# RWKV-7 stage of a two-layer trunk: sample states in four transfers each way, systems loaded one item earlier, a third raw weight buffer, and another order within a step

## The chip, the cores and the metric

The kernel runs on one core of a Trainium2 chip. The metric is the device time of one execution in microseconds (us); the smaller the better. Times of several runs are given by their median. A core has TensorE (PE in the profile; its weight loads are PEld), VectorE (DVE), ScalarE (ACT), GpSimd (POOL) and SyncE (SP). In this kernel SP does nothing but issue DMAs, one after the other in the order of its queue, and an entry whose data or buffer isn't ready holds up all that stand behind it.

## The reference

One inference step of a two-layer trunk, for a prompt of 1024 tokens with 16 learned ones ahead of it, and for 8 samples of 8 tokens each that continue from stored states. Each layer is x = x + mixer(rmsnorm(x)). Layer 0 is a gated DeltaNet. Layer 1, in which the change lies, is RWKV-7 time mixing, 16 heads of 64:

```
xs = xn + (xprev - xn) * mu                      # six mixes of a token with the one before
r, k, v, z = xs[:4] @ w_rkvz
w = -softplus(-(w0 + tanh(xs[4] @ w1) @ w2)) - 0.5 ;  a = sigmoid(a0 + (xs[5] @ a1) @ a2)
kk = l2norm(k * k_k) ;  k = k * (1 + (a - 1) * k_a) ;  decay = exp(-exp(w)) ;  b = kk * a
for each token t, each head:                     # state S is [value, key]
    S = S * decay_t + (S @ -kk_t) b_t^T + v_t k_t^T
    y_t = S @ r_t
y = groupnorm(y) * lnx_w + lnx_b + sum(r * k * r_k) * v
out = (y * silu(z)) @ w_o
```

The final states are outputs too: one for the prompt (p_rwkv) and one for each sample (s_rwkv, 8 samples x 16 heads x 64 x 64 numbers).

## The kernel before

The tokens of both inputs stand in 1104 columns, cut into three segments of 384, 384 and 336; the 64 sample tokens are the first chunk of segment 0. Float32 matmuls are split: a value x becomes a high part (a cast on ACT, "whi" or "yh", line 86) and a low part (a subtraction on POOL, "wlo" or "yl", line 90), and three matmuls take the place of one.

The last stage of the program, `wave`, runs the recurrence of layer 1 with its output projection. It starts at about 1857 us and goes on to the end. Its unit is an item: n = 8s + p, segment s and pair of heads p, 24 in all, each with 6 chunks of 64 tokens. A loop over steps tau starts a new item every second step; an item is active for six steps, so three items are worked on at a time. A step does, for the chunks of the active items: the part that depends on the old state (`step_solve`, which ends with X on DVE, line 1497, and its copy on ACT, line 1499), the solve by the chunk's precomputed triangular system (`step_inner`, matmuls rX and rS from X and rTT), then `step_old`, `step_state` (new state, output y) and the statistics of y. Between them `fill` puts matmuls that don't depend on the recurrence: the gate projection z (zz, layer 1's w_z) at first, then the output projection (zo and do, with w_o) of finished segments.

Each item is prepared by `rwkv_front`, ahead of its steps: input loads (tau = 2n-5), decays (2n-4), a third part in which r*k*r_k is split (2n-3), and six "parts" with scores, keys, values and the bonus term (2n-2 and 2n-1). The item's systems come from memory into rTT, 128 x 384 numbers, by one DMA (line 1360), which is issued with the values part at tau = 2n-1, into one of three buffers, n mod 3; the item's first use of it is at tau = 2n.

The eight items of segment 0 hold the samples as their first chunk. `rwkv_sample_read` loads the pair's 8 x 2 states (sn, eight DMAs of 64 x 2 x 64, line 1608), transposes them on PE (dsn), copies them to Sb on ACT, multiplies them with the chunk's vectors (drsr) and copies the transposed product on DVE (xss, line 1631), which X needs. `rwkv_sample_write` masks the chunk's vectors (ue, line 1638), multiplies (drsw, line 1643), adds that to Sb and scales it on DVE (lines 1645 and 1646), transposes back (dsbT), copies (ssn, ACT) and stores with eight DMAs (line 1656). The PSUM tiles of dsn, drsr, drsw and dsbT share one pool of two buffers ("d"); the second drsr group is in one of its own and the first shares the tile of the first product.

Weights of the gate and output projections come through `stream`: 72 chunks of up to 512 x 128, loaded five ahead into two raw buffers (wraw, line 204), split into whi and wlo three ahead.

`rwkv_finish` normalises y (the four and two ACT operations at line 62 of "y"), transposes it (fyT), adds the bonus and multiplies by the gate (k and lz on DVE, lines 1587 and 1588) and splits the result (yh, yl) for the projection, in pieces that `wave` calls at tau-6, tau-7 and tau-8.

On PE and ACT the instructions stand in the order in which the code is written (`manual_schedule`). On DVE, POOL and SP a planner sets the order from the dependences and its own estimates.

Of the kernel before, what the change touches and what calls it, by code (L numbers as in the profile page):

```python
# [35 lines left out]
class Builder:  # L36
# [8 lines left out]
    def t(self, pool, shape, tag, bufs=1, dt=F32):  # L45
        self.uid += 1
        return pool.tile(shape, dt, name=f"{tag}_{self.uid}", tag=tag, bufs=bufs)
# [144 lines left out]
    def open_weights(self, ctx):  # L192
        self.wp = ctx.enter_context(self.tc.tile_pool(name="weights", bufs=1))

    def load_w(self, src, kt=8, into=None, later=False):

        nc = self.nc
        n = src.shape[1]
        v = src.rearrange("(k p) m -> p k m", p=128)
        his, los = [], []  # L200
        for h in range(0, kt, 4):
            w = self.t(self.wp, [128, 4, 128], "wraw", 2)
            m = min(4, kt - h)
            nc.sync.dma_start(w[:, 0:m, 0:n], v[:, h:h + m, :])
            if later:
                return w, m, n
            if into:
                hi, lo = into[0][h // 4], into[1][h // 4]
            else:
                hi = self.t(self.wp, [128, 4, 128], "whi", 3, F32R)  # L210
                lo = self.t(self.wp, [128, 4, 128], "wlo", 3, F32R)
            self.split(w[:, 0:m, 0:n], hi[:, 0:m, 0:n], lo[:, 0:m, 0:n], eng_lo="dve" if into else "pool")
            his.append(hi)
            los.append(lo)
        return his, los

    def stream(self, srcs):

        raw, w = [], []
        for n in range(len(srcs)):  # L220
            while len(raw) < min(n + 5, len(srcs)):
                q = len(raw)
                if q > 1 and len(w) < q - 1:
                    x, m, c = raw[len(w)]
                    hi, lo = (self.t(self.wp, [128, 4, 128], a, 3, F32R) for a in ("whi", "wlo"))
                    self.split(x[:, 0:m, 0:c], hi[:, 0:m, 0:c], lo[:, 0:m, 0:c])
                    w.append((hi, lo))
                raw.append(self.load_w(srcs[q], srcs[q].shape[0] // 128, later=True))
            while len(w) < min(n + 3, len(srcs)):
                x, m, c = raw[len(w)]  # L230
                hi, lo = (self.t(self.wp, [128, 4, 128], a, 3, F32R) for a in ("whi", "wlo"))
                self.split(x[:, 0:m, 0:c], hi[:, 0:m, 0:c], lo[:, 0:m, 0:c])
                w.append((hi, lo))
            yield w[n]
# [1114 lines left out]
    def rwkv_front(self, p, s):  # L1349

        nc, t, ap, fp, col = self.nc, self.t, self.ap, self.fp, self.pcol
        P = Ctx()
# [3 lines left out]

        P.TT = self.TTz[P.n % len(self.TTz)]

        def system():
            nc.sync.dma_start(P.TT.rearrange("p c k -> p (c k)"), self.ttd[(P.n + 1) // 5][:, 384 * (P.n - max(5 * ((P.n + 1) // 5) - 1, 0)):][:, 0:384])  # L1360
        ld = self.rwkv_load(P.n, fp, "f", ("2c", "rv"))
        AR = P.AR = t(fp, [128, 2, 6, 64], "AR", NB + 1)
        BK = t(fp, [128, 6, 2, 64], "BK", 2)
# [14 lines left out]
        flat = lambda x: x.rearrange("p x k -> p (x k)")  # L1378
        yield P

        pr = t(fp, [128, 384], "pr", 1)
        with self.tc.issue_after(last):
            nc.vector.scalar_tensor_tensor(pr, ld["r"], pc("rwkv_r_k"), k2, op0=ALU.mult, op1=ALU.mult)
# [36 lines left out]
        def values():  # L1420
# [3 lines left out]
            for a in (0, 1):  # L1424
                first = (2 * P.n + a) % self.RING
                u = 0
                while u < 3:
# [4 lines left out]
                                   vp[64 * a:64 * a + 64, 128 * u:128 * u + 128 * m] if m == 1 else  # L1432
                                   vp[64 * a:64 * a + 64, 128 * u:128 * u + 128 * m].rearrange("p (c k) -> p c k", k=128))
                    u += m
        P.parts = [[lambda: scores(0)], [bonus], [lambda: keys(0)], [lambda: scores(3)], [system, values], [lambda: keys(3)]]
        if s == 0:
            read = self.rwkv_sample_read(P)
            next(read)
# [161 lines left out]
    def rwkv_sample_read(self, P):  # L1600

        nc, t, ap = self.nc, self.t, self.ap
        p, AR = P.p, P.AR
        st = self.i["state_rwkv"][0].rearrange("(g u) h v k -> u v g h k", u=2)
        sn = t(self.fin, [128, 4, 2, 64], "sn", 1)
        for u in (0, 1):
            for g in range(4):
                nc.sync.dma_start(sn[64 * u:64 * u + 64, g], st[u][:, g, 2 * p:2 * p + 2, :])
        yield
        sp = self.ps("d", 2, "sn")  # L1610
        for g in range(4):
            self.transpose(sp[:, 128 * g:128 * g + 128], sn[:, g].rearrange("p h k -> p (h k)"))
        P.Sb = t(self.fin, [128, 8, 64], "Sb", 3)
        nc.scalar.copy(P.Sb.rearrange("p b k -> p (b k)"), sp)
        yield
        rp = self.ps("d", 2, "rsr")
        for b in range(8):
            for h in (0, 1):
                a = 64 * h
                self.mm(rp[a:a + 64, 16 * b:16 * b + 16], P.Sb[a:a + 64, b, :], AR[a:a + 64, :, 0, 8 * b:8 * b + 8])  # L1620
        q = t(ap, [128, 2, 8, 8], "rkst", 1)
        nc.vector.tensor_copy(q, rp[:, 0:128].rearrange("p (b x r) -> p x b r", b=8, x=2))
        yield
        rs = [rp, self.ps("d", 2, "rsr")]
        for x in (0, 1):
            for h in (0, 64):
                g = 64 - h if x else h
                self.mm(rs[x][g:g + 64, 128:192], q[h:h + 64, x].rearrange("p b r -> p (b r)"), self.ident[h:h + 64, h:h + 64])
        P.xs = t(ap, [128, 2, 64], "xss", 3)
        for x in (0, 1):  # L1630
            nc.vector.tensor_copy(P.xs[:, x], rs[x][:, 128:192])

    def rwkv_sample_write(self, p, P, BT, DC):
        nc, t, ap = self.nc, self.t, self.ap
        UV = self.ring_uv(2 * P.n)[:, 2]
        ue = [t(self.fin, [128, 8, 64], "ue", 2) for h in (0, 1)]
        for h, e in ((0, nc.gpsimd), (1, nc.vector)):
            e.tensor_tensor(ue[h], UV[:, h, :].unsqueeze(1).broadcast_to([128, 8, 64]),
                            self.bmask.unsqueeze(2).broadcast_to([128, 8, 64]), op=ALU.mult)
        yield  # L1640
        ps = self.ps("d", 2, "rsw")
        for h in (0, 1):
            self.mm(ps[64 * h:64 * h + 64, :], BT[:, 0, 64 * h:64 * h + 64], ue[h].rearrange("p b k -> p (b k)"))
        p8 = ps.rearrange("p (b k) -> p b k", k=64)
        nc.vector.tensor_tensor(P.Sb, P.Sb, p8, op=ALU.add)
        nc.vector.tensor_tensor(P.Sb, P.Sb, DC[:, 6:14].unsqueeze(2).broadcast_to([128, 8, 64]), op=ALU.mult)
        yield
        op = self.ps("d", 2, "sbT")
        for g in range(4):
            self.transpose(op[:, 128 * g:128 * g + 128], P.Sb[:, 2 * g:2 * g + 2, :].rearrange("p b k -> p (b k)"))  # L1650
        so = t(self.fin, [128, 4, 2, 64], "ssn", 1)
        nc.scalar.copy(so.rearrange("p g h k -> p (g h k)"), op)
        st = self.o["s_rwkv"][0].rearrange("(g u) h v k -> u v g h k", u=2)
        for u in (0, 1):
            for g in range(4):
                nc.sync.dma_start(st[u][:, g, 2 * p:2 * p + 2, :], so[64 * u:64 * u + 64, g])  # L1656


    def project_out(self, s, yo, pairs, tag, ws, x2=None):
# [164 lines left out]
    def layer1(self, ctx, right, stay, xa, xb, x):  # L1824

        nc, tc = self.nc, self.tc
# [26 lines left out]
        self.UVs = t(ap, [128, self.RING, 3, 2, 64], "UV")  # L1853
        self.UVf = self.UVs.rearrange("p r c h k -> p (r c h k)")
        self.ys = t(ap, [128, self.RING, 3, 64], "y")
        self.TTz = [t(ap, [128, 6, 64], f"rTT{q}") for q in range(3)]
        nc.vector.memset(self.UVs, 0.0)
        with tc.manual_schedule(engines={mybir.EngineType.PE, mybir.EngineType.Activation}):
            self.wave(zin, stay, last, pool)
# [4 lines left out]
    def wave(self, zin, stay, last, pool):  # L1864
# [3 lines left out]
        nc, t = self.nc, self.t  # L1868
        P, x2 = {}, []
# [63 lines left out]
        for tau in range(-3, 55):  # L1933
# [12 lines left out]
            with self.tc.issue_after(ins) if W else ExitStack():  # L1946
                if W:
                    self.step_old(W)
                if 0 <= (tau - 6) // 2 < 24:
                    next(P[(tau - 6) // 2].done)  # L1950
                for f in begun:
                    next(f)
                begun.clear()
                if tau % 2 == 0 and 0 <= (tau - 8) // 2 < 24:
                    next(P[(tau - 8) // 2].done, None)
                fill(tau + 0.5)
                for f in parts[1]:
                    f()
                for Q, ci in items:
                    if ci == 1 and Q.s == 0:  # L1960
                        late.append(self.rwkv_sample_write(Q.p, Q, Q.BT, Q.DC))
                late = [x for x in late if not next(x, True)]
                if W:
                    self.step_state(W)
                fill(tau + 1)
                for f in parts[2]:
                    f()
                late = [x for x in late if not next(x, True)]
                if tau % 2 and 0 <= (tau - 7) // 2 < 24:
                    next(P[(tau - 7) // 2].done)  # L1970
                if W:
                    self.y_stats(items, tau)
                for Q, ci in items:
                    if ci == 5:
                        Q.done = self.rwkv_finish(Q.p, Q.s, Q)
                        next(Q.done)
                if tau % 2:
                    load((tau + 5) // 2)
                else:
                    front()  # L1980
# [31 lines left out]
```

## Time and profile before

| | us |
|---|---|
| median of 3 runs | 2326.65 |
| lowest and highest | 2324.69 and 2329.08 |
| profiled execution | 2324.47 |
| its span, first to last instruction | 2322.5 |
| PE busy in it | 2144.8 (92%) |
| DVE, ACT, POOL busy | 1594.6, 1271.5, 924.5 |
| mean granted TensorE clock | 0.968 of full speed |

Rows of the profile read like this. Groups and instructions: line, engine, operation, out<-in by the program's names, and at the end in brackets how long the engine had been idle ahead of it and what ended that ("<-DVE xss" is the instruction that released it). Waits: who waited for whom, us in total, how often, the longest. Stretches (a:b): the length, busy time of PE, PEld, DVE, ACT and POOL with the number of instructions, then the granted clock, the busy share of the DMA engines and GB/s. SPq rows are DMAs that SP issues, with the time that the issue took. Busy time is no bound by itself: a wait counts where it ends last.

### The profile page before, as it was taken

The page shows a single profiled execution, that of the slowest core. Times are in us where ns is not written, and L with a number is a line of the kernel's source. Part 1 is how long each engine was busy: PE and PEld are TensorE (multiplying, and loading weights), DVE is VectorE, ACT ScalarE, POOL GpSimd, SP SyncE. Part 2 cuts the span into 40 slices and gives each one's busy share as a digit, 9 for nine tenths or more (in the row PEclk, how much of TensorE's full clock was granted, in tenths as well). Part 3 has the DMA queues.
Part 4 walks back from the last instruction along what each step waited for, and adds up shares of the span by engine and source line. Part 5 has one row for each costly group of instructions (what it writes and reads, how often), then busy time and mean ns, then how long its engine had stood idle before and what let it go on. Part 6 is the DMA issues. An engine that isn't in the chain of part 4 may idle for free. (4 is left out here: it accounts for less than half of the span.)

```text
span 2322.5 us, 55260 instructions
## 1 busy us (share of the span) xinstructions
PE 2144.8 (92%) x20452; PEld 1955.3 (84%) x20452; DVE 1594.6 (69%) x4224; ACT 1271.5 (55%) x3642; POOL 924.5 (40%) x1267
## 2 busy tenths in 40 slices
PE   6989999999999999999999989998889998999995
PEld 5888988989898888988999989888878976788874
DVE  6868768686768778695335765878978355767754
ACT  5445556455555556466433554746645355677763
POOL 3435344343434334444241442544434343444433
PEclk9999999999999999999999999998989999999998
DMA  3323333323334333427244146654552554677753
GB/s 115 100 76 107 80 89 87 109 66 92 95 89 114 85 87 81 113 70 209 69 125 117 61 114 206 197 187 143 166 144 80 176 140 131 184 226 230 223 149 119
DMA packets 433127, 293.36 MB, mean 126 GB/s; under 512 B 148329, under 2 KB 415706, under 8 KB 432858
## 3 DMA queue, kind: packets, MB, share of 16 engines
q1 hardware_dynamic: 432858, 289.84, 43.5%
q8 instruction: 161, 2.64, 0.5%
q14 instruction: 108, 0.88, 0.1%
HBM read 198.02 MB, written 91.71 MB: 125 GB/s over the span
## 5 line engine op out<-in xcount | busy, mean ns | idle before, releaser
L90 POOL TENSOR_TENSOR wlo<-wraw,whi 128x512 fp32r<-128x512 f32 (+2 forms) x252 | 328.2, 1305 | 363.3 <-ACT whi L86 347.3
L76 PE MATMUL d<-xc,whi 128*128 128x384 f32 (+2 forms) x910 | 263.0, 345 | 7.0 <-DVE key L1187 2.1
L86 ACT CAST whi<-wraw 128x512 fp32r<-128x512 f32 (+2 forms) x252 | 151.8, 604 | 115.7 <-PE dq L76 50.5
L434 DVE SCALAR_TENSOR_TENSOR cvy<-raw,cw,cvy 128x408 f32<-128x408 f32 (+2 forms) x288 | 179.3, 636 | 17.6 <-ACT cvy L62 15.8
L76 PEld LDWEIGHTS d<-xc,whi 128*128 128x128 f32 (+1 forms) x910 | 170.7, 194 | 14.4 <-issue 3.8
L472 DVE TENSOR_TENSOR invT<-invT,invtmp 72x31 f32<-72x31 f32 (+31 forms) x403 | 173.1, 430 | 6.7
L470 DVE TENSOR_TENSOR invtmp<-invA,invT 72x31 f32<-72x31 f32 (+31 forms) x403 | 165.4, 410 | 11.9 <-DMA invA<-ltd 5.1
L76 PE MATMUL dz<-xc,whi 128*128 128x384 f32 (+1 forms) x480 | 148.3, 340 | 0.0
L76 PE MATMUL dv<-xc,whi 128*128 128x384 f32 (+1 forms) x480 | 146.7, 335 | 0.0
L76 PE MATMUL d<-xc,wlo 128*128 128x384 f32 (+2 forms) x428 | 145.6, 346 | 0.5 <-POOL wlo L90 0.5
L76 PE MATMUL d<-xa,whi 128*128 128x384 f32 (+3 forms) x450 | 140.4, 345 | 2.3 <-DVE key L1187 0.9
L834 POOL TENSOR_SCALAR Sb<-Sb,eglb 128x128 f32<-128x128 f32 x128 | 80.5, 646 | 91.6 <-DMA Sb<-in_state_gdn 23.1
L76 PE MATMUL dv<-xa,whi 128*128 128x384 f32 (+1 forms) x288 | 100.0, 347 | 0.1
L76 PE MATMUL dz<-xa,whi 128*128 128x384 f32 (+1 forms) x288 | 99.6, 346 | 0.0
L76 PEld LDWEIGHTS d<-xa,whi 128*128 128x128 f32 (+1 forms) x450 | 83.9, 191 | 6.8 <-issue 2.4
L76 PEld LDWEIGHTS dz<-xc,whi 128*128 128x128 f32 x480 | 88.7, 190 | 0.8
L76 PEld LDWEIGHTS dv<-xc,whi 128*128 128x128 f32 x480 | 88.5, 188 | 0.5 <-issue 0.4
L76 PE MATMUL d<-xh,wlo 128*128 128x384 f32 (+1 forms) x256 | 85.1, 346 | 2.0 <-POOL wlo L90 2.0
L62 ACT ACTIVATE o<-rA,gcol 128x128 f32<-128x128 f32 x128 | 46.7, 372 | 73.3 <-DVE S L745 72.8
L76 PE MATMUL d<-xl,whi 128*128 128x384 f32 (+1 forms) x256 | 84.9, 347 | 1.9 <-DVE xl L90 1.3
L76 PE MATMUL d<-xh,whi 128*128 128x384 f32 (+1 forms) x256 | 85.3, 346 | 0.4 <-ACT xh L86 0.2
L76 PE MATMUL d<-xa,wlo 128*128 128x384 f32 (+3 forms) x252 | 85.4, 339 | 0.0
(512 smaller groups left out, 6986.8 us busy)
## 6 DMA issues: line engine op xcount, KB each, us to landing
wraw<-in_gdn_w_in SPq DMA_DIRECT2D x96, 256.0 KB
wraw<-in_rwkv_w_rkvz SPq DMA_DIRECT2D x80, 256.0 KB
Sb<-in_state_gdn SPq DMA_DIRECT2D x64, 256.0 KB
sldcak<-cakd SPq DMA_DIRECT2D x24, 576.0 KB
cakd<-ev SPq DMA_DIRECT2D x56, 192.0 KB
wraw<-in_rwkv_w_o SPq DMA_DIRECT2D x40, 256.0 KB
E<-drow SPq DMA_DIRECT2D x24, 384.0 KB
attn<-drow SPq DMA_DIRECT2D x24, 384.0 KB
```

The source lines that it names most:

```text
L62: return self.nc.scalar.activation(out, in_, func, bias=bias, scale=scale, **kw)
L76: self.nc.tensor.matmul(out, lhsT, rhs, start=start, stop=stop)
L86: nc.scalar.copy(hi, x)
L90: e.tensor_tensor(lo, x, hi.bitcast(F32), op=ALU.subtract)
L434: nc.vector.scalar_tensor_tensor(y[:, 0:wd], raw[:, k:k + wd], cw[k], y[:, 0:wd], op0=ALU.mult, op1=ALU.add)
L470: nc.vector.tensor_tensor(tmp, A[:, j, j + 1:32].unsqueeze(2).broadcast_to([nb, n, m]), Tv[:, j, 0:m].unsqueeze(1).broadcast_to([nb, n, m] ...
L472: nc.vector.tensor_tensor(Tv[:, j + 1:32, 0:m], Tv[:, j + 1:32, 0:m], tmp, op=ALU.subtract)
L834: nc.gpsimd.tensor_scalar(Sb[:, u], Sb[:, u], self.eglb[:, hv, 4 * g + u:4 * g + u + 1], None, op0=ALU.mult)
```

## The change

Four things are changed, all of them for the last stage.

1. Sample states: each item's load and store are four DMAs of 64 x 4 x 64 (one for each parity of the sample and each head) instead of eight of 64 x 2 x 64 (each parity and each of four samples). The bytes and the contiguous pieces of 256 bytes are the same.
2. Systems: rTT has four buffers, n mod 4, and its load is issued in the third part of the item's preparation at tau = 2n-3, two steps ahead of where it stood.
3. Raw weights: a third raw buffer, which every third chunk uses, in the memory pool `fin`; chunks are loaded six ahead. The split of a chunk still stands just ahead of the load that reuses its buffer.
4. Order in a step: the split of yh and yl (`done` at tau-8) now stands ahead of the four normalisations of y (`done` at tau-6); the sample write's phases stand ahead of the preparation's third part, the filler and parts[1], and directly behind `step_state`, ahead of the second filler and parts[2].

```
-    def load_w(self, src, kt=8, into=None, later=False):
+    def load_w(self, src, kt=8, into=None, later=False, pool=None):
...
-            w = self.t(self.wp, [128, 4, 128], "wraw", 2)
+            w = self.t(self.wp if pool is None else pool, [128, 4, 128], "wraw", 2 if pool is None else 1)
...
-            while len(raw) < min(n + 5, len(srcs)):
+            while len(raw) < min(n + 6, len(srcs)):
                 q = len(raw)
-                if q > 1 and len(w) < q - 1:
+                if q > 2 and len(w) < q - 2:
...
-                raw.append(self.load_w(srcs[q], srcs[q].shape[0] // 128, later=True))
+                raw.append(self.load_w(srcs[q], srcs[q].shape[0] // 128, later=True, pool=self.fin if q % 3 == 2 else None))
...
-        def system():
-            nc.sync.dma_start(P.TT.rearrange("p c k -> p (c k)"), self.ttd[(P.n + 1) // 5][:, 384 * (P.n - max(5 * ((P.n + 1) // 5) - 1, 0)):][:, 0:384])
...
         yield P
 
+        nc.sync.dma_start(P.TT.rearrange("p c k -> p (c k)"), self.ttd[(P.n + 1) // 5][:, 384 * (P.n - max(5 * ((P.n + 1) // 5) - 1, 0)):][:, 0:384])
         pr = t(fp, [128, 384], "pr", 1)
...
-        P.parts = [[lambda: scores(0)], [bonus], [lambda: keys(0)], [lambda: scores(3)], [system, values], [lambda: keys(3)]]
+        P.parts = [[lambda: scores(0)], [bonus], [lambda: keys(0)], [lambda: scores(3)], [values], [lambda: keys(3)]]
...
         for u in (0, 1):
-            for g in range(4):
-                nc.sync.dma_start(sn[64 * u:64 * u + 64, g], st[u][:, g, 2 * p:2 * p + 2, :])
+            for h in (0, 1):
+                nc.sync.dma_start(sn[64 * u:64 * u + 64, :, h], st[u][:, :, 2 * p + h, :])
...
         for u in (0, 1):
-            for g in range(4):
-                nc.sync.dma_start(st[u][:, g, 2 * p:2 * p + 2, :], so[64 * u:64 * u + 64, g])
+            for h in (0, 1):
+                nc.sync.dma_start(st[u][:, :, 2 * p + h, :], so[64 * u:64 * u + 64, :, h])
...
-        self.TTz = [t(ap, [128, 6, 64], f"rTT{q}") for q in range(3)]
+        self.TTz = [t(ap, [128, 6, 64], f"rTT{q}") for q in range(4)]
...
                     self.step_old(W)
+                if tau % 2 == 0 and 0 <= (tau - 8) // 2 < 24:
+                    next(P[(tau - 8) // 2].done, None)
                 if 0 <= (tau - 6) // 2 < 24:
                     next(P[(tau - 6) // 2].done)
-                for f in begun:
-                    next(f)
-                begun.clear()
-                if tau % 2 == 0 and 0 <= (tau - 8) // 2 < 24:
-                    next(P[(tau - 8) // 2].done, None)
-                fill(tau + 0.5)
-                for f in parts[1]:
-                    f()
                 for Q, ci in items:
                     if ci == 1 and Q.s == 0:
                         late.append(self.rwkv_sample_write(Q.p, Q, Q.BT, Q.DC))
                 late = [x for x in late if not next(x, True)]
+                for f in begun:
+                    next(f)
+                begun.clear()
+                fill(tau + 0.5)
+                for f in parts[1]:
+                    f()
                 if W:
                     self.step_state(W)
+                late = [x for x in late if not next(x, True)]
                 fill(tau + 1)
                 for f in parts[2]:
                     f()
-                late = [x for x in late if not next(x, True)]
```

What this moves on the engines, at three places. Rows that stand together are counted (x7).

First SP's queue at the fifth sample item, before, from the load of a tile of k, a and decay inputs (fld2c, line 1254) to the load of a system:

```order
L1254 DMA fld2c_4203_24328<-cakd_95 128x2x384
L1608 DMA sn_4188_24241<-in_state_rwkv 64x2x64
L1025 DMA zd_97<-zst_4156_24092 128x336
L1656 DMA out_s_rwkv<-ssn_4161_24112 64x2x64 x8
L204 DMA wraw_4165_24141<-in_rwkv_w_rkvz 128x4x128
L1608 DMA sn_4188_24241<-in_state_rwkv 64x2x64 x7
L1360 DMA rTT0_3974_23338<-ttd_98 128x384
```

and in the changed program, from the same kind of row to a system load:

```order
L1254 DMA fld2c_4205_24304<-cakd_95 128x2x384
L1254 DMA fldrv_4147_24020<-rvd_96 128x2x384
L204 DMA wraw_4142_23993<-in_rwkv_w_rkvz 128x4x128
L1363 DMA BK_4149_24023<-abd_99 128x6x64
L1655 DMA out_s_rwkv<-ssn_4159_24075 64x4x64 x4
L1025 DMA zd_97<-zst_4160_24087 128x336
L1607 DMA sn_4192_24226<-in_state_rwkv 64x4x64 x2
L204 DMA wraw_4167_24121<-in_rwkv_w_rkvz 128x4x128
L1607 DMA sn_4192_24226<-in_state_rwkv 64x4x64 x2
L1362 DMA AR_4207_24308<-abd_99 128x384
L1379 DMA rTT0_3974_23338<-ttd_98 128x384
```

Before, the system load behind these transfers is item 3's (into rTT0, 3 mod 3); now at this place stands item 4's (into rTT0, 4 mod 4), and item 3's is in the queue already at the stage's start. State stores and loads have half as many entries.

Second PE's queue in a step of a sample item, before: the end of `step_old` and `step_state` (rY), a filler of zz matmuls for the gate, the transpose of the next keys (fBT), the two groups of drsr, and the state write drsw:

```order
L80 MATMUL rY_4173_24173<-UV_3972_23336,G_4078_23721 64x64 x2
L76 MATMUL zz_4162_24136<-xa_9_103,whi_4137_24000 128x336
L76 MATMUL zz_4162_24136<-xa_9_103,wlo_4138_24001 128x336
L76 MATMUL zz_4162_24136<-xa_9_103,whi_4137_24000 128x336 x2
L76 MATMUL zz_4162_24136<-xa_9_103,wlo_4138_24001 128x336
L76 MATMUL zz_4162_24136<-xa_9_103,whi_4137_24000 128x336
L73 MATMUL fBT_4195_24297<-ident_5_74,BK_4095_23796 128x128 x3
L76 MATMUL drsr_4178_24201<-ident_5_74,rkst_4179_24218 64x64 x2
L76 MATMUL drsr_4196_24302<-ident_5_74,rkst_4179_24218 64x64 x2
L76 MATMUL drsw_4198_24310<-ue_4190_24265,BT_4079_23722 64x512
L76 MATMUL drsw_4198_24310<-ue_4191_24266,BT_4079_23722 64x512
```

and in the changed program:

```order
L80 MATMUL rY_4175_24153<-UV_3972_23336,G_4082_23722 64x64 x2
L76 MATMUL drsw_4194_24261<-ue_4184_24212,BT_4083_23723 64x512
L76 MATMUL drsw_4194_24261<-ue_4185_24213,BT_4083_23723 64x512
L76 MATMUL zz_4164_24116<-xa_9_103,whi_4140_23989 128x336
L76 MATMUL zz_4164_24116<-xa_9_103,wlo_4141_23990 128x336
L76 MATMUL zz_4164_24116<-xa_9_103,whi_4140_23989 128x336 x2
L76 MATMUL zz_4164_24116<-xa_9_103,wlo_4141_23990 128x336
L76 MATMUL zz_4164_24116<-xa_9_103,whi_4140_23989 128x336
L73 MATMUL fBT_4198_24278<-ident_5_74,BK_4097_23788 128x128 x3
L76 MATMUL drsr_4180_24181<-ident_5_74,rkst_4181_24198 64x64 x2
L76 MATMUL drsr_4199_24283<-ident_5_74,rkst_4181_24198 64x64 x2
```

The two drsw matmuls have moved ahead of the filler, fBT and drsr.

Third ACT's queue near the end of the program, before: the copy of a chunk's y, four normalisations of y, the cast yh, the copy of a final prompt state and the cast of a weight chunk:

```order
L62 ACTIVATE y_3973_23337<-y_3973_23337,gnm_5495_30594,grs_5488_30570 128x64 x2
L1549 COPY y_3973_23337<-rY_5515_30678 128x64
L62 ACTIVATE y_3973_23337<-y_3973_23337,gnm_5533_30746,grs_5531_30739 128x64 x4
L86 CAST yh_5534_30752<-lz_5486_30567 128x336
L1596 COPY so_5537_30758<-fsT_5536_30756 64x128
L86 CAST whi_5538_30761<-wraw_5480_30529 128x384
```

and in the changed program:

```order
L62 ACTIVATE y_3973_23337<-y_3973_23337,gnm_5501_30542,grs_5490_30509 128x64 x2
L1548 COPY y_3973_23337<-rY_5517_30617 128x64
L86 CAST yh_5535_30682<-lz_5488_30506 128x336
L1595 COPY so_5538_30688<-fsT_5537_30686 64x128
L62 ACTIVATE y_3973_23337<-y_3973_23337,gnm_5539_30694,grs_5533_30678 128x64 x4
L86 CAST whi_5540_30700<-wraw_5470_30414 128x384
```

The cast yh and the copy of the state stand ahead of the four normalisations now. The numbers of instructions on PE, ACT, DVE and POOL are the same in both programs; POOL's order is the same too. On DVE the two operations on Sb (lines 1645 and 1646) stand ahead of the copies xss in the sample items, where they stood between xss and X.

## The prediction

> **What bounds the kernel now.** I read the busy times first, then three stretches of the last stage (the sample items, the prompt items, the end), and then what TensorE waits for in each.
>
> ```profile
> span 2322.5 us, 55260 instructions
> PE 2144.8 (92%) x20452; PEld 1955.3 (84%) x20452; DVE 1594.6 (69%) x4224; ACT 1271.5 (55%) x3642; POOL 924.5 (40%) x1267
> 1857.00:2030.00 173.00, 154.16 (x2190) 128.86 (x2189) 109.74 (x357) 95.52 (x267) 69.04 (x78) 0.95 0.55 151
> 2030.00:2240.00 210.00, 199.42 (x3230) 170.49 (x3230) 139.69 (x509) 153.42 (x460) 91.32 (x99) 1.00 0.72 214
> 2240.00:2322.50 82.50, 56.63 (x552) 48.38 (x548) 38.42 (x124) 33.29 (x103) 29.00 (x34) 0.87 0.42 130
> ```
>
> The columns of a stretch are its length, the busy times of PE, PEld, DVE, ACT and POOL, then the granted clock. TensorE bounds the program, and no matmul is added or removed, so the change can only win where PE stands still or runs at a lower clock: 173.0 − 154.2 = 18.8 us idle at clock 0.95 in the first stretch, 10.6 us at full clock in the second, 25.9 us at 0.87 in the third. Up to some 1850 us both programs issue the same. The profiled execution took 2324.47 us (span 2322.5), 2.2 us below the median 2326.65 of runs from 2324.69 to 2329.08; 0.2%, 4.7 us, is about what a measurement of this kernel can tell from no change.
>
> PE's waits, first in the sample stretch, then (the fourth row) in the prompt stretch:
>
> ```profile
> PE drsw L76 <- DVE xss L1631: 5.5, 7, 1.1
> PE rX L80 <- DMA rTT<-ttd: 5.2, 4, 3.1
> PE zz L76 <- DVE zst L1003: 4.3, 2, 3.4
> ...
> PE rX L80 <- DMA rTT<-ttd: 1.1, 2, 0.8
> ```
>
> Each of the first three is touched: 15.0 of the 18.8 us.
>
> **System loads and sample transfers.** SP's queue ahead of the longest stall, its state DMAs' times over the whole trace (minimum/median/maximum in ns), and PE and the clock afterwards:
>
> ```profile
> 1907.81 6.47 SPq L1656 DMA_DIRECT2D out_s_rwkv<-ssn  x8
> ...
> 1914.96 5.63 SPq L1608 DMA_DIRECT2D sn<-in_state_rwkv  x7
> 1920.70 0.54 SPq L1360 DMA_DIRECT2D rTT<-ttd  x1
> ...
> 1940.02 0.45 SPq L1360 DMA_DIRECT2D rTT<-ttd  x1
> ...
> L1608 SPq DMA_DIRECT2D sn<-in_state_rwkv x64: 597/606/1680, 1853.9 to 1977.1; - x64
> L1365 SPq DMA_DIRECT2D BK<-abd x24: 370/408/2147, 1841.8 to 2203.0; - x24
> ...
> 1923.35 0.36 PE L80 MATMUL rX<-X,rTT 64*64 64x64 f32 x1 [3.12 <-DMA rTT<-ttd]
> ...
> 1923.00:1930.00 7.00, 6.65 (x45) 5.82 (x47) 3.03 (x7) 4.12 (x12) 1.04 (x1) 0.53 0.72 208
> 1963.00:1965.00 2.00, 1.53 (x10) 1.30 (x9) 1.18 (x4) 1.08 (x5) 0.70 (x1) 0.67 0.87 231
> ```
>
> From 1907.8 to 1920.7 SP issues nothing but state stores, a weight chunk and state loads; the system load comes behind them and PE stands 3.12 us. In the changed order a system load stands at the same place of SP's queue, but it is that of the next item, two steps before its need. The next item's load here started 19.3 us later, so that is about the lead it gains, against a lateness of 3.1 us at most, so the wait goes: −5.2 here and −1.1 among the prompt items. The load still waits for the last matmul on the buffer, four items back now and one item earlier in the program, which is the same step as before: nothing is queued behind a longer wait.
>
> Behind the stall PE ran 7 us at 0.53: 7 × 0.47 = 3.3 us lost. From 1963 to 1967, after a stall for the same load of only 0.5 us, the row shows 0.67; over 4 us I count 1.7 us lost, and since other stalls stand beside that one I take half. Clock: −3.3 − 0.8 = −4.1. The Trainium skill ("TensorE: Matmul & The Clock Gate", Part 1: The HAM clock gate) halves the clock after an idle window of about 3.4 us and restores it after as long of work; the row at 1963 shows a lower clock behind shorter stalls. By the page alone the second part would be 0 and the term −3.3.
>
> Per sample item SP issues 16 state DMAs, 16 × 0.61 = 9.7 us, and 8 now. The trace has no 64x4x64 DMA. The nearest rows are 0.37 us (BK, six pieces per partition) and 0.61 us (two pieces), or 1.2 us if the time went by the pieces. I take 0.65, since the form differs from the two-piece one in one number; then 8 × 0.65 = 5.2 us, 4.5 us less per item. With the loads ahead this frees SP and ends no PE wait beyond those counted: 0. At 1.2 us SP stays as full as it is, at 0.37 it has 7 us to spare.
>
> **State update ahead of the filler.** One sample item, PE and then DVE:
>
> ```profile
> 1936.42 0.49 PE L73 MATMUL fBT<-ident,BK 128*128 128x128 f32 x3
> 1936.84 0.34 PE L76 MATMUL drsr<-ident,rkst 64*64 64x64 f32 x8
> 1938.24 1.08 PE L76 MATMUL drsw<-ue,BT 128*64 128x512 f32 x4 [1.05 <-DVE xss L1631]
> ...
> 1937.88 0.35 DVE L1631 COPY xss<-drsr 128x64 f32<-128x64 f32 x2
> 1940.10 0.68 DVE L1645 TENSOR_TENSOR Sb<-Sb,drsw 128x512 f32<-128x512 f32 x1
> 1940.82 0.69 DVE L1646 TENSOR_TENSOR Sb<-Sb,DC 128x512 f32<-128x512 f32 x1
> 1941.95 0.21 DVE L1497 TENSOR_TENSOR X<-rX,xss 128x64 f32<-128x64 f32 x1
> ```
>
> The state write drsw needs a PSUM buffer that the second drsr group holds until xss is copied, and PE stands 1.05 us, 7 times: 5.5 us. In the changed order drsw stands ahead of six zz matmuls, fBT and drsr, so its buffer is free. The second drsr must now wait until DVE has read drsw (0.68 us); between them PE has zz, fBT and the first drsr, about 1.5 us, which cover it if DVE begins at once. On DVE the two Sb operations, 1.4 us, move from just before X to before xss, which takes them out of X's way unless they hold up xss. Ends: −5.5 and +1; I take −4.5, as the cover is twice the operation. The read-out (dsbT, 4 transposes) also moves ahead and is the same work: 0.
>
> **Third raw buffer.** The start of the stage (the old second load, the load that the chain goes through, the last projection matmul, the stall), and waits for raw chunks (ACT in the sample stretch, PE at the end):
>
> ```profile
> 1851.89 0.38 SPq L204 DMA_DIRECT2D wraw<-in_rwkv_w_rkvz  x1
> 1857.25 3.13 DMA wraw<-in_rwkv_w_rkvz
> 1853.85 0.34 PE L76 MATMUL d<-xl,whi 128*128 128x384 f32 x1
> 1862.05 0.65 PE L76 MATMUL zz<-xa,whi 128*128 128x336 f32 x1 [3.37 <-DVE zst L1003]
> ...
> ACT whi L86 <- DMA wraw<-in_rwkv_w_rkvz: 5.2, 3, 2.9
> PE do L76 <- ACT whi L86: 1.4, 2, 1.1
> ```
>
> PE's stall of 3.37 us hangs on the fourth chunk, issued at 1857.25 and landed 3.1 us later; ACT casts it before the tanh. Now that chunk takes the place at 1851.89, and the third waits for its new buffer, whose memory PE still uses up to the projection's last matmul at 1854.2; with the same 3.1 us it lands near 1857.5. The cast and the tanh then end 1 to 2 us earlier: −1.5 (ends −3, and +2 if the new buffer is later). Elsewhere the loads gain a chunk's time, and of the 1.4 us at the end I take −1.0.
>
> **The y split first.** The step in the last stretch where it matters most (DVE, POOL, ACT, ACT, PE, POOL, then the clock):
>
> ```profile
> 2277.39 0.57 DVE L1588 SCALAR_TENSOR_TENSOR lz<-k,lnb,lz 128x336 f32<-128x336 f32 x1
> 2277.51 1.65 POOL L102 TENSOR_TENSOR grs<-va,cvals 128x6 f32<-128x6 f32 x1 [3.46 <-DVE va L1571]
> 2279.99 1.43 ACT L62 ACTIVATE y<-y,gnm,grs 128x64 f32<-128x64 f32 x4 [4.75 <-DVE gnm L1576]
> 2281.33 0.45 ACT L86 CAST yh<-lz 128x336 fp32r<-128x336 f32 x1
> 2281.84 0.65 PE L76 MATMUL do<-yh,whi 128*128 128x336 f32 x1 [4.44 <-ACT yh L86]
> 2281.86 0.90 POOL L90 TENSOR_TENSOR yl<-lz,yh 128x336 fp32r<-128x336 f32 x1 [2.71 <-ACT yh L86]
> 2282.00:2288.00 6.00, 5.67 (x20) 5.31 (x21) 1.01 (x2) 1.38 (x3) 3.73 (x4) 0.50 0.25 71
> ...
> 2237.82 0.42 PE L76 MATMUL zo<-yh,whi 128*128 128x336 f32 x1 [1.54 <-ACT yh L86]
> 2239.00:2243.00 4.00, 4.00 (x36) 3.72 (x36) 1.83 (x10) 0.84 (x2) 2.25 (x2) 0.65 0.59 166
> ```
>
> ACT waits 4.75 us for the normalisation's statistics and only then casts yh, though its input lz is done at 2277.96. With yh first, PE can begin at about 2278.4; yl follows when POOL is done with grs, at 2279.16, and ends at 2280.1 instead of 2282.76: 2.7 us earlier. The stretch behind it lost 6 × 0.5 = 3.0 us to the clock; as the gap is now split in two, I take half: −1.5. ACT's y comes later by yh's 0.45 us and a small copy, with a step to spare, but the next weight cast stays behind y's statistics, so I count −4.0 of these −4.2 (ends −6 and −1). The same at 2237: yh earlier by the 1.42 us of y, −1.5, and half of 4 × 0.35 = 1.4, −0.7. In the other prompt items PE is fed and it gives 0.
>
> **The sum.** Sample items −5.2 − 4.1 − 4.5, start −1.5; prompt items −1.1 − 1.5 − 0.7; end −4.0 − 1.0: −23.6 us. The waits next in line (X's chain through DVE and ACT, yl on POOL, weight casts) give some back; the sample stretch had 3.8 of 18.8 us in other waits, a fifth, and with the same again for waits not seen yet I take a quarter, +5.9. That leaves −17.7: 2324.47 − 17.7 = 2306.8 for an execution like the profiled one, and 2326.65 − 17.7 = 2309 against the median.
>
> **Rivals.** *The four-piece transfer costs double.* For it: nothing shows that form. Against it: BK with six pieces is cheaper. SP stays full, loads of raw chunks and states come late by what they do now, and only the system loads, half the clock and the end remain: −6.3 − 2.1 − 2 = −10, 2316. *Another wait takes over.* For it: ACT and DVE form one chain from rX to X and back in every step, and a PE that arrives earlier waits there. Then the 15.0 us are mostly renamed and the end's 5 us stay: 2322. *Slower:* the Sb operations hold up xss. If DVE takes drsw late, the second drsr waits for its buffer, then xss and X stand behind it: 1.4 us in each of 8 items, +11, the 4.5 us are not won, and short stalls bring the low clock as at 1963, 8 × 0.8 = +6; with −6.3 from the loads and half of the −8.7 at start, prompt yh and end, −4.4, that is +7 or 2333. It decides once the second drsr starts over 1.5 us after drsw's end. Against it: DVE is 63% busy there (109.74 of 173).
>
> **How the numbers follow.** Forecast 0.57 (2301 to 2315 its own range), double cost 0.16, renamed waits 0.15 (half of it within 0.2%, since 2322 is that bound), slower 0.12. So faster by over 0.2% 0.80, within 0.2% 0.08, slower 0.12. The range goes from the sum without give-back (2303) and the lower ends of the unknown costs, 2299, up to the renamed waits and a little over, 2325.
>
> **What would show it.** Right: no PE wait on the system load, the clock near 1.0 after 1923, drsw without a wait on xss and no wait of drsr, the state DMAs at 0.6 to 0.7 us, the zz stall below 2.5 us, PE's yh wait at the end below 1.5 us. Wrong: state DMAs of 1.2 us, PE waits on drsr, X or weight casts that add up to over 10 us, or a zz stall above 3.4 us.

## The result, and the profile after

The changed kernel's median is 2302.88 us (6 runs, 2295.82 to 2307.15) against 2325.71 us for the kernel before (6 runs, 2321.49 to 2334.09). The ratio is 0.9895, 95% interval 0.9871 to 0.9919: faster by 1.05%; the medians lie 22.8 us apart. The forecast was 2309 us, 17.7 us of gain, range 2299 to 2325.

The profiled execution took 2307.15 us, the slowest of the six. The span and busy time, then three stretches of the last stage, then PE's waits: two of the first stretch, two of the second, one of the third (columns as in the prediction):

```profile
span 2305.4 us, 55177 instructions
PE 2139.7 (93%) x20452; PEld 1951.4 (85%) x20452; DVE 1587.1 (69%) x4224; ACT 1272.0 (55%) x3642; POOL 923.8 (40%) x1267
1857.00:2030.00 173.00, 164.97 (x2431) 139.03 (x2431) 117.58 (x388) 107.23 (x302) 77.51 (x86) 0.99 0.65 184
2030.00:2240.00 210.00, 197.93 (x3150) 170.94 (x3150) 134.06 (x500) 147.80 (x442) 89.13 (x97) 0.98 0.70 207
2240.00:2305.40 65.40, 45.65 (x428) 39.10 (x424) 35.24 (x103) 28.74 (x90) 24.81 (x31) 0.85 0.43 135
...
PE zz L76 <- DVE zst L1003: 2.8, 1, 2.8
PE drsr L76 <- DVE Sb L1644: 0.8, 2, 0.6
...
PE fVT L73 <- DVE G L1408: 3.9, 2, 2.5
PE fbonus L76 <- DVE G L1408: 3.2, 1, 3.2
...
PE do L76 <- ACT yh L86: 2.1, 2, 1.6
```

The same waits of the second and third stretch before:

```profile
PE fVT L73 <- DVE G L1409: 1.2, 1, 1.2
PE fbonus L76 <- DVE G L1409: 0.5, 1, 0.5
...
PE do L76 <- ACT yh L86: 6.0, 2, 4.4
```

Neither the system load rTT nor drsw behind xss is among the waits now; in the first stretch PE is idle 8.0 us instead of 18.8, at clock 0.99 instead of 0.95. In the second it waits for G on DVE, 7.1 us instead of 1.7, and the clock there fell from 1.00 to 0.98. The stretches are cut at the same times in both profiles, so they don't hold quite the same work.

To compare stages, the last stage is counted from its first gate matmul to the end of the span. That matmul is this one before and after:

```profile
1854.03 0.31 PE L76 MATMUL zz<-xa,whi 128*128 128x336 f32 x1
```

```profile
1860.62 0.31 PE L76 MATMUL zz<-xa,whi 128*128 128x336 f32 x1
```

So the stage took 2322.5 − 1854.0 = 468.5 us before and 2305.4 − 1860.6 = 444.8 us after: 23.7 us less, while this execution had come to the stage 6.6 us later. Within the stage, the matmuls on the systems (rX from X and rTT) mark each of the 52 steps, numbered from 0. Counted from the stage's start, step 17, behind the last sample work, comes 20.6 us earlier than before; step 34 comes 19.3 us earlier, step 46 15.2, and the end 23.7. The prompt items give 5.4 us of the gain back, and the end adds 8.5.

### The profile page after: what moved, and what is told of

Its sections match the earlier page's. It is cut to its first block, busy times and chain, and to the rows that moved or that the text cites. A ratio compares the mean times of both kernels' runs of the same rounds, so it can differ in the third digit from the quotient of the medians.

```text
span 2305.4 us, 55177 instructions
## 1 busy us (share of the span) xinstructions
PE 2139.7 (93%) x20452; PEld 1951.4 (85%) x20452; DVE 1587.1 (69%) x4224; ACT 1272.0 (55%) x3642; POOL 923.8 (40%) x1267
## 5 line engine op out<-in xcount | busy, mean ns | idle before, releaser
L76 PEld LDWEIGHTS d<-xc,whi 128*128 128x128 f32 (+1 forms) x910 | 169.8, 193 | 12.5 <-issue 4.0
L62 ACT ACTIVATE attn<-attn,gcol 128x128 f32<-128x128 f32 x144 | 46.6, 390 | 71.9 <-POOL attn L545 71.8
```

The lines of the kernel that those rows point to most:

```text
L62: return self.nc.scalar.activation(out, in_, func, bias=bias, scale=scale, **kw)
L76: self.nc.tensor.matmul(out, lhsT, rhs, start=start, stop=stop)
```

## The experiments

All numbers called "stage" are counted in that way, one profile each. "Saved" is what a kernel is ahead of the kernel before, from the stage's start: at its first step, three later ones and its end. Ratios are to the kernel before, with 95% intervals.

| kernel | ratio | stage | saved at first step | step 17 | step 34 | step 46 | end |
|---|---|---|---|---|---|---|---|
| before | 1 | 468.5 | 0 | 0 | 0 | 0 | 0 |
| changed | 0.9895 (0.9871 to 0.9919) | 444.8 | 1.7 | 20.6 | 19.3 | 15.2 | 23.7 |
| changed, again | 0.9884 (0.9848 to 0.9920) | 441.8 | 0.6 | 19.4 | 24.0 | 18.9 | 26.6 |
| without four-piece transfers | 0.9944 (0.9919 to 0.9969) | 461.4 | 1.5 | 16.5 | 3.6 | −0.1 | 7.1 |
| without the early system load | 0.9873 (0.9843 to 0.9903) | 441.3 | 2.3 | 23.5 | 22.9 | 18.7 | 27.1 |
| the same, again | 0.9891 (0.9857 to 0.9926) | 439.8 | 2.6 | 23.9 | 23.2 | 20.9 | 28.6 |
| without the third raw buffer | 0.9912 (0.9878 to 0.9946) | 446.8 | −1.3 | 20.0 | 23.0 | 16.9 | 21.7 |
| without the new order | 0.9922 (0.9898 to 0.9946) | 447.1 | 1.9 | 14.0 | 17.7 | 16.2 | 21.4 |
| sample write late, yh first | 0.9888 (0.9869 to 0.9907) | 446.3 | 1.2 | 14.0 | 18.7 | 13.5 | 22.1 |
| sample write early, yh not first | 0.9862 (0.9847 to 0.9876) | 442.2 | 0.6 | 18.1 | 21.6 | 21.2 | 26.2 |
| before, only four-piece transfers | 0.9933 (0.9914 to 0.9952) | 461.5 | 0.1 | 11.0 | 10.2 | 7.0 | 7.0 |
| before, only the early system load | 0.9955 (0.9936 to 0.9974) | 463.0 | −0.7 | 8.5 | 9.8 | 2.8 | 5.5 |
| changed, five f2k buffers | 0.9866 (0.9832 to 0.9900) | 431.7 | 2.0 | 20.9 | 25.4 | 26.8 | 36.8 |
| without the early load, five f2k buffers | 0.9892 (0.9860 to 0.9924) | 446.2 | 0.3 | 21.6 | 13.1 | 14.4 | 22.3 |

The two profiles of the changed kernel differ by 1.2 us at step 17 and by 4 to 5 us from step 34 on. So a microsecond or two tells something in the sample items, but not behind them, unless the profile shows which wait made it. A profile is also one execution out of several, and not always a typical one: that of the kernel without four-piece transfers is the slowest of ten (15.0 us above the median), that with only the early load the slowest of ten too (10.0 above); with five f2k buffers, that of the changed kernel is the fastest of five (6.2 below) and that without the early load the slowest of five (8.0 above).

**State transfers and system load, each undone.** The edits, in the changed kernel (the store of the state likewise in the first):

```
-            for h in (0, 1):
-                nc.sync.dma_start(sn[64 * u:64 * u + 64, :, h], st[u][:, :, 2 * p + h, :])
+            for g in range(4):
+                nc.sync.dma_start(sn[64 * u:64 * u + 64, g], st[u][:, g, 2 * p:2 * p + 2, :])
```

```
-        nc.sync.dma_start(P.TT..., self.ttd...)          # in the third part of the preparation
+        P.parts = [..., [system, values], ...]            # in the values part, two steps later
-        self.TTz = [t(ap, [128, 6, 64], f"rTT{q}") for q in range(4)]
+        self.TTz = [t(ap, [128, 6, 64], f"rTT{q}") for q in range(3)]
```

> The changed kernel with the state transfers put back to 8 + 8 of 64x2x64. The last stage (first gate matmul behind the projections to the end) took 468.5 us before and 444.8 us in the changed kernel's profile. Theory (the system load's lead removed the wait, the number of transfers only freed SP): stage 445 to 449, no PE wait on the system load above 0.5 us in all. Rival (the shorter SP queue removed it): PE waits 3 to 6 us for system loads again, low clock behind them, stage 453 to 457.

> The changed kernel with the system load put back to the values part, one step ahead of its use, into three buffers. Theory (the lead did it): PE waits 3 to 6 us for system loads, low clock behind the longest, stage 451 to 456. Rival (the shorter SP queue did it: half the state DMAs end the load's lateness of 3.1 us by themselves): no such wait above 1 us in all, stage 445 to 447.

Without the four-piece transfers no PE wait on a system load came back: the lead does remove that wait. But against the changed kernel 4.1 us are lost by step 17 and another 11.6 by step 34 (2.9 and 17.5 against its second profile), far more than the 0 of the prediction; over the runs it is 0.9944 against 0.9895, about half a per cent, with intervals that just touch. So neither expectation was met: the stage is longer than both, by other waits. One wait of PE in that kernel's sample items that the changed kernel doesn't have, the two longest DVE waits on transfers (the whole last stage), and two rows of SP and one of the chain from where time is lost between steps 17 and 20:

```profile
PE dsn L73 <- DMA sn<-in_state_rwkv: 2.3, 7, 0.5
...
DVE zst L1679 <- DMA zst<-x1T: 12.5, 3, 6.3
DVE AR L1372 <- DMA fldrv<-rvd: 8.6, 4, 3.5
...
2021.95 5.93 SPq L1655 DMA_DIRECT2D out_s_rwkv<-ssn  x8
2032.48 0.74 SPq L1665 DMA_DIRECT2D zst<-x1T  x1
...
2032.48 7.25 DMA zst<-x1T
```

The old stores hold SP for 5.9 us; what has piled up behind them is then issued in one burst, and a load in that burst takes 7.25 us to land. DVE waits on loads of zst from x1T, which the output projection needs, in all three kernels with the old transfers (5.0 us before, 6.0 with only the early load, 12.5 here) and, but for 0.5 us without the third raw buffer, in none of the eleven profiles with four-piece ones.

Without the early load, the sample items show no wait on a system load at all, and the kernel is not slower than the changed one (0.9873 and 0.9891 against 0.9895 and 0.9884). Half the state transfers are enough to bring the load in time there. The expected cost of 6 to 11 us in the stage did not come. Behind the sample items the wait comes back, by the waits of that kernel behind 1995 us in its two profiles, and of the one with five f2k buffers that comes later:

```profile
PE rX L80 <- DMA rTT<-ttd: 4.1, 4, 2.0
```

```profile
PE rX L80 <- DMA rTT<-ttd: 5.4, 6, 1.9
```

```profile
PE rX L80 <- DMA rTT<-ttd: 9.6, 5, 3.8
```

No kernel with the early load and the shorter lists shows it.

**Each alone, on the kernel before.** The edits are those parts of the change, applied to the kernel before.

> The kernel before with only the state transfers changed to 4 + 4. Stage before 468.5 us. Theory now (SP's queue was the cause: half the state DMAs bring the system loads forward and all other loads too): PE waits on system loads fall from 6.3 to under 2 us in all, stage 454 to 459. The prediction's price of this part was 0: stage 467 to 469, waits on system loads as before.

> The kernel before with only the system load moved two steps ahead into four buffers. If the lead by itself is a cure: no PE wait on system loads, stage 457 to 461 (the prediction's 10.4 us less some give-back). If SP's queue only brings another load late instead: no such wait either, but other waits behind transfers of 4 us or more, stage 463 to 468.

PE's waits in the sample items, with only the transfers changed, and then with only the load moved:

```profile
PE drsw L76 <- DVE xss L1631: 4.4, 6, 1.1
PE zz L76 <- DVE zst L1003: 4.4, 2, 3.4
...
PE rX L80 <- DMA rTT<-ttd: 0.2, 1, 0.2
```

```profile
PE zz L76 <- DVE zst L1003: 5.2, 2, 4.2
PE drsw L76 <- DVE xss L1630: 4.4, 6, 1.1
...
PE dsn L73 <- DMA sn<-in_state_rwkv: 0.9, 3, 0.4
```

Each alone all but ends the wait on system loads in the sample items (5.2 us before). From the first step to step 17 the transfers save 10.9 us and the load 9.2; the kernel with both, but with the old order, saves 14.0 − 1.9 = 12.1. They are two cures for one illness, and their gains do not add. Behind the sample items each loses part again: with only the transfers, system loads are late once by 2.2 us near step 21 (3.8 us lost with the clock); with only the load, PE waits 5.0 us for G near step 35, behind an output store that DVE waits 4.6 us for.

**The third raw buffer undone.**

```
-            w = self.t(self.wp if pool is None else pool, [128, 4, 128], "wraw", 2 if pool is None else 1)
+            w = self.t(self.wp, [128, 4, 128], "wraw", 2)
...
-            while len(raw) < min(n + 6, len(srcs)):
+            while len(raw) < min(n + 5, len(srcs)):
```

> The changed kernel with two raw buffers and loads five chunks ahead. Theory (third buffer worth 2.5 us): stage 446 to 449, the first gate stall back at 3.4 us. Rival (the changed kernel loses 9.4 us against the kernel before between 2100 and 2150 us, in waits behind late input loads, because weight chunks loaded one further ahead stand before them): that loss is gone, stage 436 to 441.

The stall at the stage's start is back, at 4.1 us:

```profile
PE zz L76 <- DVE zst L1003: 4.1, 1, 4.1
```

The rival fell: the loss between steps 34 and 35 is there without the third buffer too. At the first step the four profiles with two buffers stand between −1.3 and 0.1 us (mean −0.5), the ten with three between 0.3 and 2.6 (mean 1.5): 2.0 us. From step 46 to the end this kernel saves 4.8 us, the changed one 8.5 and 7.7: 3.3 us. Over the runs this kernel isn't told apart from the changed one (0.9912, interval 0.9878 to 0.9946).

**The order in a step undone, whole and in its two halves.** In the whole all phases of the step stand as before. In the halves only one piece goes back:

```
 # sample write late, yh first: the yh split stays ahead, the write goes back
-                (sample write's phases)  begun  fill  parts[1]  step_state  (write)  fill  parts[2]
+                begun  fill  parts[1]  (sample write's phases)  step_state  fill  parts[2]  (write)
 # sample write early, yh not first: the write stays ahead, the yh split goes back
-                done(tau-8)  done(tau-6)  (sample write's phases)  begun  fill
+                done(tau-6)  (sample write's phases)  begun  done(tau-8)  fill
```

> The changed kernel with the old order within a step (sample write behind the filler, y's normalisations ahead of yh). Theory (order worth 4.5 us in the sample items, 2.2 among the prompt items, 4.0 at the end): stage 453 to 457, drsw waits 5 to 6 us on xss, the yh wait at the end 4 us or more. Rival (the loads alone carry the gain): stage 445 to 447.

> The changed kernel with the sample write's place in a step as before, yh's split still first. Prediction (4.5 us): drsw waits 4 to 6 us on xss, stage 448 to 451 against 444.8. Rival (DVE's and ACT's chain to X sets the step anyway): the wait is back but the stage is within 2 us of 444.8, up to the waits behind late input loads, which differ by run.

> The changed kernel with y's normalisations ahead of yh's split as before, the sample write still early. Prediction (6.2 us, 4.0 of it in the last 45 us): the yh wait at the end 4 us or more and low clock behind it, stage 449 to 452 against 444.8. Rival (weight casts and the last transfers set the end): the stage is within 2 us of 444.8.

With the write late, whole or half, step 17 comes at 14.0 us saved, against 20.6 and 19.4: the early write is worth about 6 us. Its wait is back in the half:

```profile
PE drsw L76 <- DVE xss L1630: 3.4, 5, 1.1
PE drsw L76 <- DVE bnst L1557: 1.0, 2, 0.5
```

With yh not first the old wait at the end is back, and longer than it was:

```profile
2260.70 0.65 PE L76 MATMUL do<-yh,whi 128*128 128x336 f32 x1 [4.99 <-ACT yh L86]
```

From step 46 to the end that kernel saves 5.0 us and the changed one 8.5 and 7.7, so yh first is worth some 3 us there (the whole undone saves 5.2). Still this kernel has the ratio 0.9862: it does not lose the 5 us near step 35 (21.6 saved at step 34, 21.2 at 46). Whether the order of ACT protects it there or the transfers fell well in that profile was not separated; the kernel without any of the new order loses only 1.3 us there, but the one with only the early load, in the old order too, loses 7.0.

The expected costs of the stage did not come: with the order undone whole it is 447.1 us where 453 to 457 were expected, in its halves 446.3 and 442.2 for 448 to 451 and 449 to 452. At step 46 the kernel without the new order is about where the changed one is (16.2 against 15.2 and 18.9), and that with only the write late is 1.7 and 5.4 us behind: little of what the early write saves by step 17 is sure to be left then. Nor do the runs tell any of the three apart from the changed kernel: the intervals overlap.

**The loss near step 35, and the changed kernel again.** The changed kernel there, DVE and PE, then the clock:

```profile
2137.19 1.41 DVE L1715 SCALAR_TENSOR_TENSOR f2k<-dfin,frs,fw 128x512 f32<-128x512 f32 x2 [2.75 <-DMA out_y_prompt<-f2k]
2138.51 1.01 DVE L1408 TENSOR_TENSOR G<-fG,gm 128x384 f32<-128x384 f32 x2
...
2139.11 0.69 PE L76 MATMUL fbonus<-prh,bones 128*128 128x384 f32 x1 [3.17 <-DVE G L1408]
...
2138.00:2146.00 8.00, 6.89 (x45) 6.07 (x46) 3.91 (x14) 1.75 (x5) 1.27 (x1) 0.57 0.56 173
```

DVE waits to write a tile of the final output (f2k, three buffers) until the first store of that tile has landed; G stands behind it on DVE, PE behind G, and eight microseconds at 0.57 follow. Another wait of the kind stands near step 32, where DVE waits 3.2 us for an input load that takes 7.3 us from issue to landing, by the chain and DVE's row:

```profile
2102.12 7.31 DMA fldrv<-rvd
...
2109.52 0.56 DVE L1372 TENSOR_TENSOR AR<-fldrv,fDp 128x384 f32<-128x384 f32 x1 [3.21 <-DMA fldrv<-rvd]
```

The edit for the first, in the changed kernel and in the one without the early load:

```
-            junk = t(self.fin2, [128, 512], "f2k", 3)
+            junk = t(self.fin2, [128, 512], "f2k", 5)
...
-                y = t(self.fin2, [128, 512], "f2k", 3)
+                y = t(self.fin2, [128, 512], "f2k", 5)
```

> The changed kernel once more, beside the next three on one chip. The wait of DVE on the first stores of the final output (2.7 us in the first profile) and those on late input loads fldrv (5.5 us) come back if the program causes them; if they hang on how transfers happen to fall, their sum differs by over 3 us. Stage 440 to 449.

> The kernel without the early system load once more, on the same chip as the changed kernel. If the lead is worth nothing beside the shorter transfer lists: the same time as the changed kernel within 4 us. If it costs: 3 to 6 us faster. If the first comparison was chance and the lead is still worth its forecast: 5 us or more slower.

> The changed kernel with five instead of three buffers for the final output tile f2k, so that the first stores need not land before the next tile is written. If that wait is what PE stood for near 2136 to 2139 us: no DVE wait on the store there, the loss of about 5 us in that step gone, stage 437 to 442. If another transfer takes its place: within 2 us of the changed kernel.

> The kernel without the early system load, with five buffers for f2k: stage 435 to 439, about 5 us under the kernel without the early load and the fastest here, if both losses are as read; within 2 us of it otherwise.

The wait on the store was there again in the second profile of the changed kernel (4.0 us) and in both of the kernel without the early load (2.9 and 2.1), so the program makes it. With three f2k buffers and yh first it was 2.1 to 5.7 us in all seven profiles; with the old order of yh it was 0, 0.4, 1.3, 1.7 and 4.6 us, so that order bears on it but doesn't settle it. The wait on fldrv was 5.5 us once and 0.3 the other time, so it hangs on how transfers fall. With five buffers DVE waits for no store of the output, and PE's waits from 2128 to 2150 us are all in this row:

```profile
PE fyT L76 <- ACT UV L1430: 0.2, 1, 0.2
```

The changed kernel with five buffers has the fastest median of all, 2296.34 us against 2302.24 for the changed kernel in the same comparison, and the shortest stage, 431.7 us. That is less than the 437 to 442 expected: the loss near step 35 that went is 5 to 6 us, and what else made this stage shorter wasn't looked into; the profile is of the fastest of the five runs. The intervals of the two ratios overlap (0.9832 to 0.9900 and 0.9848 to 0.9920), so by time alone it isn't shown to be the better of the two; it beats the kernel before. Without the early load the five buffers bring nothing in the times, and system loads are late by 9.6 us in all in that profile, the slowest of five: the last expectation was missed.

## Why the prediction was right or wrong

The sign and the range held, and the mechanism of most terms; 22.8 us were gained where 17.7 were forecast. That the sum came so near is in part luck: the largest cure, 9.3 us for the lead of the system load, would have been had without the lead, from the transfers that were put at 0, as the kernel without the early load shows. Of the signs that were named, the zz stall (2.8 us, for less than 2.5), the wait of drsr (0.8, for none) and the longest yh wait at the end (1.6, for less than 1.5) were missed by little. Term by term:

- *System load, −5.2 and −4.1 with the clock.* Right as a mechanism and in size: alone it saves 9.2 us between the first step and step 17, for 9.3 forecast, and the wait is gone in the changed kernel; with only the early load 5.5 us are saved at the end. The prediction counts 1.7 us of lost clock over 1963 to 1967 beside a row that covers 1963 to 1965; over the four microseconds the clock was 0.59, which makes 1.6. What the prediction missed is that the other part ends the same wait, so that beside the shorter lists the lead shows no gain in the times.
- *Four-piece transfers, 0.* This is the step that failed. Their price was right: an issue costs as much as before, by the groups of the state loads and stores in the changed kernel:

```profile
L1607 SPq DMA_DIRECT2D sn<-in_state_rwkv x32: 601/614/1890, 1861.8 to 1957.9; - x32
L1655 SPq DMA_DIRECT2D out_s_rwkv<-ssn x32: 607/615/1901, 1895.8 to 2011.3; - x32
```

  The median is 0.61 us, as for half the pieces before. What was wrong is "this frees SP and ends no PE wait beyond those counted". Alone it saves 10.9 us from the first step to step 17; beside everything else it is worth 4.1 or 2.9 us by step 17, where PE waits 2.3 us for sample states without it, and more behind it: there loads of the output projection came up to 6.3 us late without it. How much more is less certain, as the profile without it is of the slowest run; over the runs all of it is about half a per cent, 11 us. The rival of a double price fell with the same rows. (The 0.37 us for BK, taken as the cheap end, is the least of its 24 issues; the median is 0.41.)
- *State write ahead of the filler, −4.5.* Right, and too small: about 6 us. The wait that was expected in its place is there at 0.8 us, in two of eight items (drsr behind Sb):

```profile
1934.53 0.33 PE L76 MATMUL drsr<-ident,rkst 64*64 64x64 f32 x4 [0.57 <-DVE Sb L1644]
```

  So the slower rival, in which it grows to 1.4 us an item, did not occur. How much of the 6 us is left at the end is not shown.
- *Start, −1.5.* About right: 2.0 us. The stall is 2.8 us for 3.37, and the clock behind it 0.72 over six microseconds for 0.50, by these rows of the changed kernel and of the kernel before:

```profile
1868.00:1874.00 6.00, 5.90 (x34) 5.44 (x35) 1.75 (x6) 0.95 (x2) 3.42 (x3) 0.72 0.64 183
```

```profile
1862.00:1868.00 6.00, 5.95 (x26) 5.38 (x27) 1.15 (x4) 0.62 (x1) 2.68 (x3) 0.50 0.64 191
```

- *End, −4.0 for yh and −1.0 for the raw buffer; −2.2 at 2237.* From step 46 to the end these 7.2 us were 8.5 and 7.7, right in sum and wrong in parts: about 3 for yh, 3.3 for the raw buffer, the rest not told apart. PE could start yh's matmuls early, as forecast, but lz itself ended late (2.75 us of ACT's wait is for it) and yl still stood behind grs on POOL:

```profile
2266.61 0.47 ACT L86 CAST yh<-lz 128x336 fp32r<-128x336 f32 x1 [2.75 <-DVE lz L1587]
2268.69 0.65 PE L76 MATMUL do<-yl,whi 128*128 128x336 f32 x1 [0.91 <-POOL yl L90]
```

- *Give-back, +5.9.* Between steps 17 and 46 it was 5.4 us in the first profile and 0.5 in the second, so the size was met in one of two, and the place was not. The prediction looked for it in X's chain through DVE and ACT, yl and weight casts; it was waits behind transfers, the output store in both profiles and an input load in the first, and the clock behind them.
- *The clock.* In the sample stretch it rose from 0.95 to 0.99 as forecast. The Trainium skill ("TensorE: Matmul & The Clock Gate", Part 1: The HAM clock gate) names an idle window of about 3.4 us; here 3.17 us of waiting was followed by 0.57 and 2.8 us by 0.72, so waits somewhat under that length cost clock already. The stall of 3.12 us in the kernel before, with 0.53 behind it, was under it too, so that, taken strictly, that figure gives nothing for the first part of the term either, where the prediction has −3.3.

## What to carry to other kernels

When one queue issues all transfers, price the queue's time, not only the transfer that is seen to be late: halving the number of issues and moving the late load ahead each ended the same wait, and the first also kept later loads from piling up. Do not add up two parts that cure the same wait; cost each beside the other. Ask for a saving in the middle of a program whether it is still there at the end. Look for a new wait where the engine that now arrives earlier meets a buffer whose store hasn't landed, and try another copy of that buffer: here five took the wait away, though by the times alone the gain isn't shown.

## What was not expected of the hardware

A DMA of 64 x 4 x 64 took SP 0.61 us to issue, as one of 64 x 2 x 64 did, with twice the pieces. The first gate matmul, up to which the programs are the same but for a few issues on SP just ahead of it, came at times from 1853.4 to 1866.2 us in the profiles: nearly 13 us that hardly come from the change (1857.1 and 1854.1 in two profiles of one kernel, 1853.4 and 1863.4 in two with the old raw buffers), and about as much as the runs of one kernel spread (12.6 us for the kernel before). Where in the first layers they come from was not looked into.
